# More first halves of the experts ahead of the gates, their results parked in DRAM: a two-layer PEER backbone on one core

## The chip, the cores and the metric

One core of one Trainium2 chip runs the whole program in one launch. The metric is the device time of one execution in microseconds, lower is better; the time of a kernel is the median of its runs.

## What is computed

The reference is a two-layer backbone over 256 latent tokens and 256 context tokens of width 1024. Each layer has an attention mixer and then a PEER channel mixer; the change touches the PEER part alone. For each token PEER picks 8 x 16 of 16384 experts, each an input vector `u` and an output vector `v`, and a gate for each pick:

```
def peer(h, w_q, sub_keys, u, v):
    q = (h @ w_q).reshape(T, 8, 2, 128)
    s = einsum('thpd,hpnd->thpn', q, sub_keys)
    sv, si = top_k(s, 16)
    cand = sv[:, :, 0, :, None] + sv[:, :, 1, None, :]
    fv, fi = top_k(cand.reshape(T, 8, 256), 16)
    idx = i1 * 128 + i2
    g = softmax(fv)
    act = gelu(einsum('td,ted->te', h, u[idx]))
    return einsum('te,ted->td', g * act, v[idx])
```

In layer 0 it runs over all 512 tokens, in layer 1 over the 256 latent ones.

## The kernel before

The kernel does not gather the picked experts (but for one block of tokens). It computes all 16384 experts for its tokens and multiplies by a dense matrix of gates that is zero where an expert was not picked. The experts are cut into 128 blocks of 128. For block i there are two halves:

- `first(i)` (line 755 on): load `u` (512 KB), split it into a high and a low bf16 half on ACT and DVE (`halves`, lines 101 and 102), 24 matmuls into a PSUM bank `tr` (`project`, line 282), and a Gelu on ACT (line 768) that writes `ga`, the activations of 128 experts for n tokens. In layer 0 n is 384, in layer 1 it is 256.
- `second(i)` (line 770 on): load `v` (512 KB), split it (lines 775 and 776, ring `vv` of four), for every eighth block load the gates `gq` from DRAM (line 779), multiply `ga` by the gates into `wf` (DVE, line 781), split that into `wh` (ACT) and `wl` (DVE), and 18 matmuls of 512 columns (12 in layer 1) into accumulators (line 791).

A first half needs only the normed tokens `h2`. A second half needs the gates, which `dense_gates` builds (lines 728 to 744): one-hot products on DVE (`oh`, `go`), small matmuls into banks `sc` and `pv`, copies into `stage` on ACT, and a 1 MB store `gd` per 16 tokens (24 stores in layer 0, 16 in layer 1). The first half does not wait for this, so some run while DVE builds gates: `PRE` (18 in layer 0, 32 in layer 1) have a buffer of their own for `ga`, `PARKED` (10 and 16) put it into `xT`, whose content lies in DRAM for that time. The others share a ring of four buffers `ga`.

The fourth block of 128 tokens in layer 0 goes another way: 128 indirect DMAs on POOL's queue (line 908) fetch 1 MB of expert rows each, and DVE multiplies and sums them (lines 914 and 920) beside layer 0's dense stage. So do the `wm` tiles of the modulation (line 160).

No order is written by hand. A scheduler takes the program, instruction by instruction, and fixes for each engine and each DMA queue one order, in which the chip then issues; a buffer of a ring is handed on when its last reader is done. All DMAs but the indirect ones are issued by SP, one queue, in order: a DMA that waits holds those behind it. "Gates" below is the stage in which gates are built, "dense" the one that follows, until the layer's last second half.

Of the kernel before, what the change touches and what calls it, by code (L numbers as in the profile page):

```python
# [9 lines left out]
F32 = mybir.dt.float32  # L10
# [8 lines left out]
P = 128  # L19
# [29 lines left out]
def program(ctx: ExitStack, tc: tile.TileContext, a, out):  # L49
    nc = tc.nc  # L50
    V, A, T, G = nc.vector, nc.scalar, nc.tensor, nc.gpsimd

    def pool(name, stack, bufs=1, side=None):
        return stack.enter_context(tc.tile_pool(name=name, bufs=bufs, side=side, reuse_waits="tile"))
# [5 lines left out]
    def bank(tag):  # L60
        return ps.tile([P, 512], F32, name=tag, tag=tag, bufs=2)
# [31 lines left out]
    def halves(t, shape, dt, keep=None):  # L93

        if dt == BF:
            hl = wk.tile([P, 2] + shape[1:], BF, name="half", tag="half", bufs=4) if keep is None else keep
            h, l = hl[:, 0], hl[:, 1]
        else:
            h = wk.tile(shape, dt, name="half", tag="half", bufs=4)
            l = wk.tile(shape, dt, name="half", tag="half", bufs=4)  # L100
        A.activation(h, t, AF.Copy)  # L101
        V.tensor_tensor(l, t, h, op=OP.subtract)  # L102
        return h, l
# [96 lines left out]
    def advance(steps, n):  # L200
        for _ in range(n):
            next(steps, None)
# [75 lines left out]
    def project(w, src, t0, n, p):  # L278

        for c in range(NC):  # L280
            for i, j in ((0, 0), (0, 1), (1, 0)):
                T.matmul(p[:, :n], w[i][:, c], src[j][:, c, t0:t0 + n], start=(c == 0 and i + j == 0), stop=(c == NC - 1 and i == 1))  # L282
# [465 lines left out]
    def dense(layer, n, h2, gd, dp, up, pre, extra, done):  # L748
        nt = n // P
        held = []  # L750
        acc = [[bank(("pv", "sc", "mm")[t]) for _ in range(2)] for t in range(nt)]
        gas, gqs = {}, {}
        flat = xT.rearrange("p c t -> p (c t)")

        def first(i):
            u = st.tile([P, NC, P], F32, name="u4", tag="u4", bufs=RING["u4"])
            nc.sync.dma_start(u, a[f"u{layer}"][i])
            w = halves(u, [P, NC, P], BF)
            p = bank("tr")
            project(w, h2, 0, n, p)  # L760
            if i < PRE[layer]:
                gas[i] = pre.tile([P, n], F32, name=f"ga{i}")
            elif i < PRE[layer] + PARKED[layer]:
                x = i - PRE[layer]
                gas[i] = flat[:, x * n:(x + 1) * n]
            else:
                gas[i] = up.tile([P, n], F32, name="ga", bufs=4)
            A.activation(gas[i], p[:, :n], AF.Gelu)  # L768

        def second(i):  # L770
            v = st.tile([P, D], F32, name="v4", tag="v4", bufs=RING["v4"])
            nc.sync.dma_start(v, a[f"v{layer}"][i * P:(i + 1) * P])
            vv = dp.tile([P, 2, D], BF, name="vv", bufs=HELD)
            vh, vl = vv[:, 0], vv[:, 1]
            A.activation(vh, v, AF.Copy)  # L775
            V.tensor_tensor(vl, v, vh, op=OP.subtract)  # L776
            if i % OCT == 0:
                gqs[0] = dp.tile([P, n // TB, OCT, TB], F32, name="gq", bufs=2)
                nc.sync.dma_start(gqs[0], gd[:, i // OCT].rearrange("p b (i t) -> p b i t", t=TB))
            wf = dp.tile([P, n], F32, name="wf", bufs=2)  # L780
            V.tensor_tensor(wf.rearrange("p (b t) -> p b t", t=TB), gas[i].rearrange("p (b t) -> p b t", t=TB), gqs[0][:, :, i % OCT], op=OP.mult)  # L781
            wh = dp.tile([P, n], BF, name="wh", bufs=max(HELD, 3))
            A.activation(wh, wf, AF.Copy)  # L783
            wl = dp.tile([P, n], BF, name="wl", bufs=HELD)
            V.tensor_tensor(wl, wf, wh, op=OP.subtract)  # L785

            def products(t):
                s = slice(t * P, (t + 1) * P)
                for w, v in ((wh, vh), (wh, vl), (wl, vh)):
                    for x in range(2):  # L790
                        T.matmul(acc[t][x], w[:, s], v[:, x * 512:(x + 1) * 512], start=(i == 0 and w is wh and v is vh),  # L791
                                 stop=(i == NK - 1 and w is wl))

            if i < NK - HELD:
                for t in range(nt):
                    products(t)
            else:
                held.append(products)

        for i in range(NK + AHEAD):  # L800
            if i < NK:
                first(i)
            if i >= AHEAD:
                second(i - AHEAD)
                extra(i - AHEAD)

        for t in reversed(range(nt)):
            for products in held:
                products(t)
            done(t, acc[t])  # L810
# [11 lines left out]
    PRE = (18, 32)  # L822
    PARKED = (TT * NC // (3 * P), TT * NC // SEQ)
    AHEAD = 2
    HELD = 4
    MODS = (8, 112)
    LAG = 4
    GATHERED = NK - 9
# [4 lines left out]
    with ExitStack() as layer0:  # L833
# [24 lines left out]
        up = pool("up0", r0, 2, side="right")  # L858
# [67 lines left out]
        def beside(i):  # L926
# [20 lines left out]
            if FRONT <= i < NK - 2:  # L947
                with tc.high_priority():
                    advance(early[0], 1)
            if i >= MODS[0]:  # L950
                advance(steps, 80 * (i + 1 - MODS[0]) // MODS[1] - 80 * (i - MODS[0]) // MODS[1])

# [30 lines left out]
        def front_(t, acc):  # L983
            with tc.high_priority():
                front(t, acc)
        dense(0, 3 * P, h2, gd, dp, up, pre, beside, front_)
        r0.close()
        hT, keys_values, attend = f1[1:]
# [9 lines left out]
    with ExitStack() as layer1:  # L998
        keep = pool("keep1", layer1)
        up = pool("up1", layer1, 2)  # L1000
# [65 lines left out]
        def finish(t, acc):  # L1066
# [15 lines left out]
            for g, y in enumerate(ys):  # L1082
                gs = slice(g * 512, (g + 1) * 512)
                V.scalar_tensor_tensor(y, y, r, fg[:, gs], op0=OP.mult, op1=OP.mult)
                nc.sync.dma_start(out[t * P:(t + 1) * P, gs], y)

        dense(1, SEQ, h2, gd, dp, up, pre, beside, finish)


# [86 lines left out]
```

## Time and profile before

| what | us |
|---|---|
| median of 3 runs | 2619.19 (2616.99 to 2622.06) |
| the profiled execution, its own time | 2624.13 |
| its span, first to last instruction | 2622.3 |
| PE busy | 2454.3 (94%) |
| DVE busy | 2142.3 (82%) |
| ACT busy | 1218.7 (46%) |
| gates of layer 0, about | 540 to 745 |
| dense of layer 0, about | 745 to 1560 |
| gates of layer 1, about | 1937 to 2061 |
| dense of layer 1, about | 2074 to 2611 |

Times along the program are microseconds from the span's start. A view by windows gives for each stretch the busy time of each engine (with the number of its instructions), the granted clock of TensorE as a share of 2.4 GHz, the busy share of the 16 DMA engines and the rate that they moved. A matmul's weights are loaded on PEld, beside PE.

### The profile page before, as it was taken

What the parts mean: (1) busy time and instruction counts of PE and PEld (TensorE: products, weight loads), DVE (VectorE), ACT (ScalarE), POOL (GpSimd) and SP (SyncE); (2) the same over time, 40 slices, a digit from 0 to 9 for tenths busy, and PEclk for the clock granted to TensorE, in tenths of its full rate; (3) what the DMA queues carried; (4) which work ended last, traced back from release to release, by engine and by line L of the source; (5) the groups of instructions that cost most, each with busy time, mean ns of one, the idle gap of its engine ahead of it and who ended that gap; (6) DMA issues with size and microseconds to landing.
All of it is one profiled execution on the core that took longest, in us unless ns stands there. A gap on an engine that the chain in (4) does not pass through costs nothing.

```text
span 2622.3 us, 41821 instructions
## 1 busy us (share of the span) xinstructions
PE 2454.3 (94%) x15600; PEld 1570.8 (60%) x15600; DVE 2142.3 (82%) x4820; ACT 1218.7 (46%) x2117; POOL 196.4 (7%) x132
## 2 busy tenths in 40 slices
PE   6989899999679999999999998798999699999998
PEld 2866479766534555555555555667888445666665
DVE  5975649999988999999988886977998787666665
ACT  3334535445433444444443334555565445555554
POOL 0000000000000212233222210000000000000000
PEclk8989899999679999999999999999999899999999
DMA  7631205556789999999999863701578977777762
GB/s 262 213 101 33 88 36 196 163 184 190 206 323 344 344 371 376 354 407 374 372 363 349 333 228 122 237 13 59 185 221 254 320 268 259 238 231 220 234 217 80
DMA packets 221000, 614.09 MB, mean 234 GB/s; under 512 B 16758, under 2 KB 104312, under 8 KB 199804
## 3 DMA queue, kind: packets, MB, share of 16 engines
q1 hardware_dynamic: 202364, 477.19, 53.5%
q0 software_dynamic: 18432, 134.23, 13.2%
q8 instruction: 122, 2.00, 0.3%
q14 instruction: 82, 0.67, 0.1%
HBM read 565.21 MB, written 46.15 MB: 233 GB/s over the span
## 4 chain that ended last, share of the span: by engine, by line
PE 71%; DVE 19%; DMA 5%; issue 2%; ACT 2%; SPq 0%; DVEq 0%; ACTq 0%
PE tr L282 23%; PE sc L791 12%; PE pv L791 12%; PE mm L282 8%; PE mm L791 6%; DVE half L102 4%; DVE go L733 3%; PE sc L385 2%; PE tr L292 2%; DVE oh L728 1%; PE pv L549 1%; PE mm L320 1%; PE sc L320 1%; PE sc L532 1%; DMA u<-in_u 1%
## 5 line engine op out<-in xcount | busy, mean ns | idle before, releaser
L282 PEld LDWEIGHTS <-half 128*128 128x128 bf16 x7488 | 723.9, 98 | 287.6 <-issue 10.8
L282 PE MATMUL tr<-h,half 128*128 128x384 bf16 (+1 forms) x6144 | 877.7, 300 | 4.6 <-ACT xT L768 2.0
L791 PEld LDWEIGHTS <-wh 128*128 128x128 bf16 x2560 | 251.5, 98 | 315.7 <-ACT wh L783 33.5
L102 DVE TENSOR_TENSOR half<-u,half 128x1024 bf16<-128x1024 f32 (+1 forms) x300 | 365.2, 1218 | 65.8 <-ACT half L101 64.9
L775 ACT ACTIVATE vv<-v 128x1024 bf16<-128x1024 f32 x256 | 269.3, 1055 | 277.5 <-issue 73.5
L776 DVE TENSOR_TENSOR vv<-v,vv 128x1024 bf16<-128x1024 f32 x256 | 312.3, 1221 | 102.7 <-ACT vv L775 101.7
L101 ACT ACTIVATE half<-u 128x1024 bf16<-128x1024 f32 (+1 forms) x300 | 315.2, 1051 | 105.1 <-DMA u<-in_u 43.9
L791 PE MATMUL pv<-vv,wh 128*128 128x512 bf16 x1024 | 269.7, 382 | 35.2 <-ACT wh L783 32.1
L908 POOL DMA_INDIRECT uv<-in_uv,idx x128 | 196.2, 1533 | 1347.4 <-DVE wf L781 753.1
L791 PE MATMUL sc<-vv,wh 128*128 128x512 bf16 x1024 | 269.5, 382 | 0.0
L768 ACT ACTIVATE ga<-tr 128x384 f32<-128x384 f32 (+1 forms) x230 | 100.5, 437 | 317.2 <-PE tr L282 315.2
L791 PEld LDWEIGHTS <-wl 128*128 128x128 bf16 x1280 | 125.5, 98 | 153.1 <-issue 2.1
L160 DVE CUSTOM_DVE_ANT_0 junk<-wm,silu_c 128x1024 bf16<-128x1024 f32 x160 | 194.8, 1218 | 1.8 <-DMA wm<-in_w_mod 1.0
L781 DVE TENSOR_TENSOR wf<-ga,gq 128x384 f32<-128x384 f32 (+1 forms) x230 | 111.8, 490 | 96.2 <-ACT ga L768 84.1
L783 ACT ACTIVATE wh<-wf 128x384 bf16<-128x384 f32 (+1 forms) x256 | 117.9, 463 | 131.2 <-DVE wf L781 62.6
L920 DVE SCALAR_TENSOR_TENSOR acc<-uv,wgt,acc 128x1024 f32<-128x1024 f32 x127 | 162.6, 1280 | 2.0
L914 DVE CUSTOM_DVE_ANT_0 uv<-uv,ht 128x1024 f32<-128x1024 f32 x128 | 155.6, 1217 | 0.3 <-DMA uv<-in_uv,idx 0.3
L791 PE MATMUL pv<-vv,wl 128*128 128x512 bf16 x512 | 153.2, 381 | 0.9 <-DVE wl L785 0.9
L791 PE MATMUL sc<-vv,wl 128*128 128x512 bf16 x512 | 152.9, 380 | 0.0
L282 PE MATMUL mm<-h,half 128*128 128x256 bf16 (+1 forms) x1248 | 137.4, 271 | 11.1 <-ACT h L274 3.5
L282 PE MATMUL mm<-hT,half 128*128 128x512 f32 (+1 forms) x672 | 140.1, 362 | 6.6 <-ACT hT L274 3.1
L791 PE MATMUL mm<-vv,wh 128*128 128x512 bf16 x512 | 134.4, 381 | 0.0
(275 smaller groups left out, 2758.6 us busy)
## 6 DMA issues: line engine op xcount, KB each, us to landing
u<-in_u SPq DMA_DIRECT2D x256, 512.0 KB
v<-in_v SPq DMA_DIRECT2D x256, 512.0 KB
wm<-in_w_mod SPq DMA_DIRECT2D x80, 512.0 KB
gd<-stage SPq DMA_DIRECT2D x40, 1024.0 KB
gq<-gd SPq DMA_DIRECT2D x16, 1536.0 KB
gq<-gd SPq DMA_DIRECT2D x16, 1024.0 KB
u<-in_w_pq SPq DMA_DIRECT2D x24, 512.0 KB
v<-in_w_pq SPq DMA_DIRECT2D x24, 512.0 KB
```

Of the source, the lines that this page charges most:

```text
L101: A.activation(h, t, AF.Copy)
L102: V.tensor_tensor(l, t, h, op=OP.subtract)
L160: mod_last[0] = order(V.tensor_tensor_reduce(junk, w, sc[:, s], 1.0, 0.0, OP.mult, OP.add, mods[layer][:, k, j, s:s + 1]))
L282: T.matmul(p[:, :n], w[i][:, c], src[j][:, c, t0:t0 + n], start=(c == 0 and i + j == 0), stop=(c == NC - 1 and i == 1))
L775: A.activation(vh, v, AF.Copy)
L776: V.tensor_tensor(vl, v, vh, op=OP.subtract)
L781: V.tensor_tensor(wf.rearrange("p (b t) -> p b t", t=TB), gas[i].rearrange("p (b t) -> p b t", t=TB), gqs[0][:, :, i % OCT], op=OP.mult)
L783: A.activation(wh, wf, AF.Copy)
L791: T.matmul(acc[t][x], w[:, s], v[:, x * 512:(x + 1) * 512], start=(i == 0 and w is wh and v is vh), stop=(i == NK - 1 and w is wl))
L908: dma = G.indirect_dma_start(out=uv[:], out_offset=None, in_=a["uv0"], in_offset=bass.IndirectOffsetOnAxis(ap=idx[:, k:k + 1], axis=0))
L914: keep_order(V.tensor_tensor_reduce(uv[:, :D], uv[:, :D], ht, 1.0, 0.0, OP.mult, OP.add, act3[:, k:k + 1]))
L920: V.scalar_tensor_tensor(acc3, uv[:, D:], wgt3[:, k:k + 1], acc3, op0=OP.mult, op1=OP.add)
```

## The change

After the `PRE` and `PARKED` blocks, the next 16 first halves of layer 0 and the next 8 of layer 1 no longer leave their result in the ring until their second half: it is stored to a DRAM tile `sent` right after the Gelu, and `second(i)` reads the result of block i + 1 back into a buffer of the same ring of four.

```
--- before.py
+++ after.py
@@ dense
         flat = xT.rearrange("p c t -> p (c t)")
+        sent = tc.dram_tile([P, SENT[layer], n], F32, name=f"sent{layer}")
 
         def first(i):
...
             else:
                 gas[i] = up.tile([P, n], F32, name="ga", bufs=4)
             A.activation(gas[i], p[:, :n], AF.Gelu)
+            x = i - PRE[layer] - PARKED[layer]
+            if 0 <= x < SENT[layer]:
+                nc.sync.dma_start(sent[:, x], gas.pop(i))
 
         def second(i):
+            x = i + 1 - PRE[layer] - PARKED[layer]
+            if 0 <= x < SENT[layer]:
+                gas[i + 1] = up.tile([P, n], F32, name="ga", bufs=4)
+                nc.sync.dma_start(gas[i + 1], sent[:, x])
             v = st.tile([P, D], F32, name="v4", tag="v4", bufs=RING["v4"])
...
     HELD = 4
+    SENT = (16, 8)
```

So blocks 28 to 43 of layer 0 (196,608 bytes each way) and 48 to 55 of layer 1 (131,072 bytes each way) take the new path: 24 stores and 24 read-backs on SP's queue. Lines from 754 on stand 1 to 9 further down in the changed kernel (768 becomes 769, 772 becomes 780).

What the scheduler made of it is seen at three places. The first is ACT in the gates of layer 0, where the last Gelus ahead of the dense stage stand (`stage` is a copy of gates, `half` the split of a `u`). Before, the fourth and last buffer of the ring is `ga_8638`, the result of block 31:

```order
L768 ACTIVATE ga_8638<-tr_8613 128x384
L101 ACTIVATE half_8893<-u4_8891 128x1024
L743 ACTIVATE stage_5730<-sc_5767 128x128x4
L743 ACTIVATE stage_5730<-pv_5777 128x128x4
L743 ACTIVATE stage_5806<-sc_5812 128x128x4
L743 ACTIVATE stage_5806<-pv_5822 128x128x4
L101 ACTIVATE half_8964<-u4_8962 128x1024
L101 ACTIVATE half_9039<-u4_9037 128x1024
L743 ACTIVATE stage_5806<-sc_5837 128x128x4
L743 ACTIVATE stage_5806<-pv_5847 128x128x4
```

With the change, the same place (`ga_8646` is block 31, `ga_8716` block 32):

```order
L769 ACTIVATE ga_8646<-tr_8621 128x384
L101 ACTIVATE half_8913<-u4_8911 128x1024
L743 ACTIVATE stage_5730<-sc_5767 128x128x4
L743 ACTIVATE stage_5730<-pv_5777 128x128x4
L743 ACTIVATE stage_5806<-sc_5812 128x128x4
L743 ACTIVATE stage_5806<-pv_5822 128x128x4
L769 ACTIVATE ga_8716<-tr_8691 128x384
L101 ACTIVATE half_8987<-u4_8985 128x1024
L101 ACTIVATE half_9065<-u4_9063 128x1024
L743 ACTIVATE stage_5806<-sc_5837 128x128x4
L743 ACTIVATE stage_5806<-pv_5847 128x128x4
```

One more Gelu stands there, and none follows until the dense stage. Counted over the whole of ACT's order, 33 Gelus now stand ahead of the last `stage` copy of layer 0 where 32 stood, and 53 where 52 stood in layer 1; one split of a `u` (lines 101 and 102) and one group of 24 matmuls per layer move with them.

The second place is SP's queue at the same time. With the change, from the second of these stores on (the numbers on `ga` tell buffers apart: 8500 is written by block 29, 8568 by 30, 8646 by 31, 8716 by 32; 8571, 8649 and 8719 are read back for blocks 29, 30 and 31, and block 28 was read back just before):

```order
L772 DMA sent0_6697<-ga_8500 128x384
L744 DMA gd0_4093<-stage_5660 2048x1x128
L758 DMA u4_8985<-in_u0 128x1024
L778 DMA ga_8571<-sent0_6697 128x384
L772 DMA sent0_6697<-ga_8568 128x384
L772 DMA sent0_6697<-ga_8646 128x384
L778 DMA ga_8649<-sent0_6697 128x384
L744 DMA gd0_4093<-stage_5730 2048x1x128
L758 DMA u4_9063<-in_u0 128x1024
L758 DMA u4_9137<-in_u0 128x1024
L772 DMA sent0_6697<-ga_8716 128x384
L778 DMA ga_8719<-sent0_6697 128x384
```

Five stores and four read-backs stand in the gates of layer 0 between the `gd` stores and `u` loads that stood there alone. The four read-backs (blocks 28 to 31) take all four buffers of the ring, long before their second halves come.

The third place is SP in the dense stage of layer 0, about where second halves 23 to 29 are worked off. Before (`v4_8500` is the `v` of block 27):

```order
L171 DMA wm_10458<-in_w_mod 128x1024
L772 DMA v4_8431<-in_v0 128x1024
L772 DMA v4_8500<-in_v0 128x1024
L772 DMA v4_8565<-in_v0 128x1024
L171 DMA wm_10606<-in_w_mod 128x1024
L171 DMA wm_10819<-in_w_mod 128x1024
L772 DMA v4_8640<-in_v0 128x1024
L772 DMA v4_8707<-in_v0 128x1024
```

With the change (`v4_8505` is the `v` of block 27, `ga_8791` the result of block 33, `ga_8794` block 32 read back):

```order
L772 DMA sent0_6697<-ga_8791 128x384
L780 DMA v4_8433<-in_v0 128x1024
L780 DMA v4_8505<-in_v0 128x1024
L171 DMA wm_10655<-in_w_mod 128x1024
L780 DMA v4_8573<-in_v0 128x1024
L778 DMA ga_8794<-sent0_6697 128x384
L171 DMA wm_10868<-in_w_mod 128x1024
L772 DMA sent0_6697<-ga_8869 128x384
L778 DMA ga_8872<-sent0_6697 128x384
L780 DMA v4_8651<-in_v0 128x1024
L780 DMA v4_8721<-in_v0 128x1024
L772 DMA sent0_6697<-ga_8941 128x384
```

The other 11 stores (blocks 33 to 43) and 12 read-backs (32 to 43) of layer 0 stand here, among the `v` loads; in layer 1 three stores and four read-backs stand in the dense stage.

## Rows read from the trace of the kernel before

**Rows 1.** The page's parts 1 and 2, whole span.

```profile
PE 2454.3 (94%) x15600; PEld 1570.8 (60%) x15600; DVE 2142.3 (82%) x4820; ACT 1218.7 (46%) x2117; POOL 196.4 (7%) x132
PE   6989899999679999999999998798999699999998
...
DVE  5975649999988999999988886977998787666665
...
PEclk8989899999679999999999999999999899999999
```

**Rows 2.** Windows by stage: busy us of each engine, clock, DMA share, GB/s.

```profile
core 0: us, PE busy (x) PEld busy (x) DVE busy (x) ACT busy (x) POOL busy (x), PEclk, DMA share, GB/s
...
650.00:745.00 95.00, 55.12 (x489) 43.76 (x487) 88.17 (x229) 39.00 (x65) 0.00 (x0) 0.66 0.73 216
...
850.00:1150.00 300.00, 300.00 (x1599) 156.28 (x1598) 299.60 (x456) 125.60 (x205) 79.35 (x48) 1.00 0.95 368
1150.00:1560.00 410.00, 410.00 (x2214) 216.44 (x2212) 366.41 (x521) 163.94 (x288) 108.62 (x73) 1.00 0.92 351
1990.00:2055.00 65.00, 58.41 (x603) 51.78 (x601) 57.87 (x93) 36.70 (x64) 0.00 (x0) 0.93 0.85 264
2055.00:2075.00 20.00, 3.45 (x35) 2.38 (x35) 7.22 (x13) 7.08 (x12) 0.00 (x0) 0.67 0.89 304
...
2300.00:2600.00 300.00, 299.64 (x2087) 204.65 (x2085) 180.83 (x232) 154.07 (x231) 0.00 (x0) 1.00 0.65 208
```

**Rows 3.** Waits of PE in the dense stage of layer 0, 750 to 1560.

```profile
PE pv L791 <- DVE vv L776: 1.7, 1, 1.7
PE pv L791 <- ACT vv L775: 1.2, 1, 1.2
```

**Rows 4.** Windows of 10 us, the same columns.

```profile
660.00:670.00 10.00, 5.41 (x67) 4.53 (x65) 10.00 (x20) 4.09 (x7) 0.00 (x0) 0.81 0.81 240
...
760.00:770.00 10.00, 10.00 (x48) 4.50 (x46) 9.87 (x16) 4.70 (x6) 0.00 (x0) 1.00 1.02 412
...
840.00:850.00 10.00, 8.26 (x41) 3.88 (x40) 10.00 (x16) 2.65 (x5) 2.68 (x2) 1.00 0.82 283
...
940.00:950.00 10.00, 10.00 (x58) 5.44 (x56) 10.00 (x20) 4.07 (x9) 1.40 (x1) 1.00 1.02 423
```

**Rows 5.** Waits in the gates of layer 0, 540 to 748 (total, times, longest).

```profile
PEld L741 <- DVE go L733: 30.5, 23, 9.3
...
PE pv L791 <- ACT wh L783: 14.7, 1, 14.7
...
ACT stage L743 <- DMA gd<-stage: 6.3, 3, 2.7
```

**Rows 6.** Costliest groups by form, whole span: the split of `u`.

```profile
L102 DVE TENSOR_TENSOR half<-u,half 128x1024 bf16<-128x1024 f32 x280 | 340.7, 1218 | 57.7 <-ACT half L101 56.7 <-issue 0.4
```

**Rows 7.** SP's issues at the end of layer 0's gates, in order of time.

```profile
728.21 4.54 SPq L744 DMA_DIRECT2D gd<-stage  x2
732.91 2.05 SPq L130 DMA_DIRECT2D silu_c<-silu  x1
738.11 0.81 SPq L779 DMA_DIRECT2D gq<-gd  x2
```

**Rows 8.** Waits around the end of layer 1's gates, 2000 to 2110.

```profile
PE pv L791 <- ACT wh L783: 16.0, 1, 16.0
...
DVE wf L781 <- DMA gq<-gd: 8.1, 1, 8.1
...
ACT stage L743 <- DMA gd<-stage: 6.0, 2, 4.0
```

**Rows 9.** Waits in the dense stage of layer 0, 870 to 1010.

```profile
ACT vv L775 <- DMA v<-in_v: 9.4, 7, 4.0
ACT vv L775 <- PE mm L791: 8.4, 7, 2.1
DVE uv L914 <- DMA uv<-in_uv,idx: 0.3, 1, 0.3
```

## The prediction

> **What bounds the kernel now.** I read the page's busy rows and slices first, then windows by stage, then who waits in each. PE is busy 94% of the span at a granted clock near full, and its slices of 65.6 us dip, beside the start and layer 1's attention (slices 25 to 28), in slices 11 and 12, the end of layer 0's gates, and in slice 32, the end of layer 1's [rows 1]. So the question is one of stages. In the dense stage of layer 0 PE is busy without a gap from 850 on, at 2.4 GHz (clock 1.00) [rows 2], and between 750 and 1560 it waits 2.9 us in all [rows 3]. That stage is bound by PE. DVE is as full there until 1150 (299.6 of 300 us), and the DMA engines are close behind with a share of 0.95 [rows 2]: three resources stand side by side, PE ahead by a little. In the gates of layer 0 it is the other way round. DVE is busy 10.00 of 10 us [rows 4], PE stands and waits for DVE's `go` (30.5 us in all) [rows 5], and from 650 to 745 PE is busy 55.12 of 95 us at a mean clock of 0.66 [rows 2]. That is the room the change aims at: a first half moved there should cost PE nothing and relieve the dense stage.
>
> **What a first half is worth.** From 1150 to 1560 PE issued 2214 matmuls, 185 ns each [rows 2]; a block has 24 + 18 = 42 of them, so 7.78 us. Second halves alone run at 48 matmuls in 10 us, 208 ns each [rows 4], so 18 take 3.75 us. The first half is the rest, 4.0 us. In layer 1 the rate is 300 / 2087 = 144 ns [rows 2], a block of 24 + 12 is 5.17 us, and both halves stream the same number of columns (24 x 256 and 12 x 512), so a first half is 2.6 us. What it costs where it goes is the split of `u` on DVE, 1.22 us [rows 6], because DVE sets the pace of the gates. The split and the Gelu on ACT lie beside that: ACT is busy 39 of 95 us [rows 2].
>
> **How many move.** The orders of the two kernels answer this, and not with 16 and 8. One Gelu more stands ahead of the last gates in each layer, 33 for 32 and 53 for 52. The reason is the ring. The read-back of block i + 1 has nothing to wait for but its store and a free buffer, so the scheduler issues the read-backs of blocks 28 to 31 inside the gates; they fill all four buffers of `ga` and keep them until second halves 28 to 31 have read them. Block 33 then has no buffer before second half 28, deep in the dense stage. The detour through DRAM gives back four of the buffers it was to save; what is gained is the one result (block 32, and 52 in layer 1) that lies in DRAM alone.
>
> **The sum.** Layer 0's dense stage loses one first half: -4.0 us. Its gates gain one split on DVE: +1.2. Layer 1's dense stage: -2.6. Its gates: +1.2, since DVE is nearly full there too (57.87 of 65 us) [rows 2].
>
> The 24 stores and 24 read-backs cost DMA time, and SP's order. In the gates of layer 0 five stores and four read-backs are 9 x 0.197 = 1.77 MB in a stretch whose DMA share is 0.73 [rows 2]: hidden in the free quarter. A read-back there holds SP until its store has landed, and a `gd` store behind it is late, which holds ACT's next `stage` copy (it waits for that 6.3 us already [rows 5]). The trace has no store of this size. The nearest is the last `gd` store, 1 MB, issued by about 732.2, after which SP could issue the `gq` load at 738.1 [rows 7], so at most 5.9 us for one. A store of gates goes out every 205 / 24 = 8.5 us, which covers such a wait. I take 0, with 5.9 as the upper end.
>
> At the end of layer 1's gates the cover is thinner. PE waits 16.0 us there for the first second half, DVE 8.1 us for `gq`, ACT 6.0 us for `gd` stores [rows 8]: the last stores end the stage. Nine transfers of 0.131 MB and one `u` of 0.52 MB come on top, 1.70 MB; the DMA engines moved 304 GB/s at a share of 0.89 there [rows 2], 342 when full, so between 0 and 5.0 us. Of these only the `u` load stands among the last three `gd` stores; I take its 1.5 us.
>
> In the dense stage of layer 0 eleven stores and twelve read-backs are 4.52 MB, and they come while second halves 28 to 45 run, some 17 blocks of 7.78 us, 132 us. At the best rate, 423 GB/s at a share of 1.02 [rows 4], they take 10.7 us of all DMA engines. The free share is 5% [rows 2], 6.6 us. So between 0 and 10.7 us. I take 0: from 870 to 1010 ACT waited 8.4 us, seven times, for PE to free a buffer of `vv` [rows 9], so `v` was up to four blocks ahead of PE, and a load that lands some us later is not yet felt. The Trainium skill (DMA: Bandwidth & Descriptors, Specifications) puts the limit from HBM at about 358 GB/s for a core. This trace disagrees: 368 GB/s over 300 us. By that figure the stage would be DMA-bound already and the whole 4.52 MB would be added, an estimated 12.6 us, against the 0 that I take.
>
> SP's order adds waits as well. The store of block 33 stands ahead of the `v` loads of blocks 26, 27 and 28, and waits for a Gelu that waits for a buffer. But that buffer is freed by `wf` of block 28, and DVE's split of `v` 23, for which the load of `v` 26 waits anyway, stands right behind it on DVE. Some tenths of a microsecond, inside the same lead of `vv`: 0. In layer 1's dense stage PE is busy 299.64 of 300 us with DVE at 180.83 and DMA at 0.65 [rows 2], so seven small transfers are hidden; the cover is DVE's free 40%.
>
> Together: -4.0 + 1.2 - 2.6 + 1.2 + 1.5 = -2.7 us. The profiled execution took 2624.13 us by its own time (span 2622.3) and would take 2621.4; it lies 4.9 above the median of the runs, 2619.19, which becomes **2616.5 us**. That is 0.1%, and about 0.2% (5.2 us) is what a measurement of this kernel can tell from no change. I forecast no change.
>
> **Rivals.** *The DMA engines fill up* (slower). The 4.52 MB find no room, `v` and gathered rows land late, and DVE, which now waits 0.3 us for a gather in 140 us [rows 9], waits for them; with DVE full there is nothing to catch up with before 1150. For it: ACT already waits 9.4 us for `v` in that stretch [rows 9]. Against it: the lead of `vv`, and windows that reach 1.02. It decides once the lead is used up. This is also what a limit of 358 GB/s would do (the Trainium skill, DMA: Bandwidth & Descriptors, Specifications), and the 368 GB/s measured speak against it. Price from the rows: the whole 10.7, so 2616.5 + 10.7 = 2627.2 us. Chance 0.22, and 0.02 more for the held SP queue in the gates on top of it (5.9 us).
>
> *PE's holes close too* (faster). Before block 34 PE has few first halves to put between seconds; from 840 to 850 it issued 41 matmuls for 48 [rows 4], and that is where its 2.9 us of waiting lie [rows 3]. In the new order one more first half is in hand there. If those waits go and the end of layer 1's gates does not suffer, 2616.5 - 2.9 - 1.5 = 2612.1 us. Against it: DVE is full right there, and a wait for it returns elsewhere. Chance 0.22.
>
> *The change does what its words say*: all 16 and 8 run ahead, 16 x (4.0 - 1.2) + 8 x (2.6 - 1.2) = 56 us, so 2563 us. PE's idle 40 us in 650 to 745 [rows 2] would allow most of it, but the order is fixed before the chip sees it: 0.02.
>
> **How the numbers follow.** No change, around 2616.5: 0.52. Faster 0.22 + 0.02 = 0.24, slower 0.22 + 0.02 = 0.24. The likeliest case alone spans 2612 to 2623 (its unknown terms: 1.5 less to 5.9 more, and the scatter of runs). The range reaches down past the closed holes and up past the full DMA engines with the held queue, 2627.2 + 5.9: 2607 to 2633.
>
> **What would show it.** Right: 33 and 53 Gelus ahead of the last `stage` copies; the first second half of layer 0 about 1 us later; PE still without waits in the dense stage, and that stage about 4 us shorter; the DMA share from 870 to 1010 near 1.00 without consequences. Wrong: waits of PE for `wh`, `vv` or `wl` between 860 and 1010, DVE idle behind a gather or `v`, SP waiting for a store while `v` loads stand behind it, or a gates stage longer by more than 2 us.

## The result, and the profile after

The changed kernel took 2637.2 us (median of 5 runs, 2632.32 to 2639.94) against 2622.06 us for the kernel before in the same session (5 runs, 2616.99 to 2625.52): a ratio of 1.0062, 95% interval [1.0051, 1.0073]. It is 0.6% slower, 15 us, where no change was forecast at 2616.5 us and the range ended at 2633. The profiled execution took 2635.86 us by its own time (span 2634.1), 11.8 us of span more than the one of before. The profile of before is of a run 2.1 us above its median and that of after of one 1.3 us below; hence 11.8 where the medians differ by 15.

Where those 11.8 us lie is read from two kinds of instruction in the timeline: the copies into `stage` (first one of each layer) and the matmuls of the second halves (first and last start of each layer). Layer 0's last second half starts at 1617.9 us before, so "dense 0" reaches past the 1560 at which the windows of [rows 2] end.

| stretch, us | before | after | difference | forecast |
|---|---|---|---|---|
| start to the first `stage` copy of layer 0 | 543.7 | 541.2 | -2.5 | 0 |
| gates 0: to the first second half | 202.5 | 203.7 | +1.2 | +1.2 |
| dense 0: to the last second half | 871.7 | 881.4 | **+9.7** | **-4.0** |
| attention of layer 1 | 321.2 | 320.1 | -1.1 | 0 |
| gates 1 | 134.9 | 140.3 | **+5.4** | **+2.7** |
| dense 1 | 537.1 | 536.2 | -0.9 | -2.6 |

The loss has two places, the dense stage of layer 0 and the gates of layer 1. The first stretch lies ahead of all that the change touches.

The page's parts 1 and 2 after, to be laid beside [rows 1]:

```profile
PE 2450.2 (93%) x15600; PEld 1568.5 (60%) x15600; DVE 2144.8 (81%) x4820; ACT 1216.9 (46%) x2117; POOL 198.5 (8%) x132
...
PE   5999899999679989999999998899999699999998
...
PEclk8989899999689999999999999999999799999999
```

PE is busy as long as before, but for 4 us. What is new is a slice of 8 at 14 (counted from 0: 922 to 988 us), in a stage where [rows 1] has a 9. The windows by stage after (the two of layer 1's gates begin 7 us later, and the second of them is 6 us longer), beside [rows 2]:

```profile
650.00:745.00 95.00, 53.78 (x495) 41.92 (x493) 88.12 (x229) 39.04 (x67) 0.00 (x0) 0.68 0.76 232
850.00:1150.00 300.00, 288.45 (x1510) 148.16 (x1509) 295.61 (x449) 118.71 (x199) 83.89 (x48) 0.99 0.95 375
1150.00:1560.00 410.00, 410.00 (x2216) 216.54 (x2214) 361.71 (x509) 162.54 (x284) 105.37 (x73) 1.00 0.92 350
1997.00:2062.00 65.00, 57.32 (x592) 51.09 (x590) 54.73 (x88) 35.32 (x61) 0.00 (x0) 0.95 0.82 256
2062.00:2088.00 26.00, 7.75 (x79) 6.14 (x77) 12.19 (x19) 9.61 (x17) 0.00 (x0) 0.59 0.97 324
2300.00:2600.00 300.00, 299.64 (x2080) 204.09 (x2079) 183.88 (x233) 155.45 (x233) 0.00 (x0) 1.00 0.68 216
```

From 850 to 1150 PE was busy all 300 us before and is busy 288.45 us now, with 1510 matmuls for 1599. The DMA share is the same 0.95. The waits of PE in the dense stage of layer 0 (750 to 1560), 2.9 us in [rows 3]:

```profile
PE pv L799 <- ACT wh L791: 11.6, 4, 4.9
PE pv L799 <- ACT vv L783: 1.2, 1, 1.2
PE tr L282 <- ACT ga L769: 0.3, 1, 0.3
```

So PE waits four times for `wh`, the high half of the gated result, which ACT makes from DVE's `wf`. The 10-us windows show where, and what DVE did meanwhile (compare 940:950 in [rows 4]):

```profile
930.00:940.00 10.00, 9.50 (x54) 5.09 (x52) 10.00 (x15) 1.69 (x4) 2.23 (x2) 1.00 1.02 424
940.00:950.00 10.00, 6.30 (x25) 2.85 (x26) 10.00 (x17) 3.90 (x7) 2.03 (x2) 0.83 1.02 417
...
980.00:990.00 10.00, 5.61 (x21) 2.42 (x22) 9.84 (x18) 3.77 (x9) 0.00 (x0) 0.83 0.91 369
```

In the windows in which PE stands, DVE is busy 10.00 and 9.84 of 10 us. It hardly waits; it is doing something else first. DVE's timeline between two `wf` (start, duration, instruction) says what:

```profile
925.08 0.55 DVE L789 TENSOR_TENSOR wf<-ga,gq 128x384 f32<-128x384 f32 x1
...
928.04 1.21 DVE L102 TENSOR_TENSOR half<-u,half 128x1024 bf16<-128x1024 f32 x1
...
930.87 1.27 DVE L929 SCALAR_TENSOR_TENSOR acc<-uv,wgt,acc 128x1024 f32<-128x1024 f32 x1
932.07 1.21 DVE L923 CUSTOM_DVE_ANT_0 uv<-uv,ht 128x1024 f32<-128x1024 f32 x1
...
934.43 1.21 DVE L102 TENSOR_TENSOR half<-u,half 128x1024 bf16<-128x1024 f32 x1
...
939.06 1.21 DVE L102 TENSOR_TENSOR half<-u,half 128x1024 bf16<-128x1024 f32 x1
940.20 1.21 DVE L160 CUSTOM_DVE_ANT_0 junk<-wm,silu_c 128x1024 bf16<-128x1024 f32 x1
...
942.54 0.54 DVE L789 TENSOR_TENSOR wf<-ga,gq 128x384 f32<-128x384 f32 x1
```

For 17.5 us, more than two blocks of 7.78 us, no `wf` comes, but three splits of `u` for first halves, and gathers (`uv`, `acc`), `wm` tiles (`junk`) and splits of `v`. Counted from 745 to 945, the groups by form of the kernel before (first) and of the changed one:

```profile
L781 DVE TENSOR_TENSOR wf<-ga,gq 128x384 f32<-128x384 f32 x32 | 17.4, 550 | 3.5 <-DMA gq<-gd 3.5
L781 DVE TENSOR_TENSOR wf<-xT,gq 128x384 f32<-128x384 f32 x10 | 5.5, 555 | 0.2
```

```profile
L789 DVE TENSOR_TENSOR wf<-ga,gq 128x384 f32<-128x384 f32 x28 | 15.2, 549 | 0.0
L789 DVE TENSOR_TENSOR wf<-xT,gq 128x384 f32<-128x384 f32 x10 | 5.5, 553 | 0.1
```

In that window 42 blocks were gated before and 38 after, at the same 0.55 us each; two more of the changed kernel's lie ahead of 745, so by 945 it is 42 against 40. The distance still grows: `wf` of block 43 starts at 956.6 us before and at 983.2 after. These instructions did not become slower; their order is another one. Summing DVE's instructions in their order, from the stage's first `wf` on, each at the mean of its row (1.22 us for a split, a `uv` and a `junk`, 1.27 for an `acc`, 0.55 for `wf` and `wl`), 232 us of work stand ahead of `wf` of block 43 before, and 260 us after. (Their own times in the two traces add up to 226 and 253 us: the same difference, but for 1 us.) PE's work ahead of that block's products (4.0 and 3.75 us a half) is 209 and 217 us. DVE is asked for 28 us more, PE for 8. In the traces the additional instructions are five splits of `u`, two of `v`, six `junk`, three `uv` and five `acc`. They came with first halves that run further ahead: at that place the splits of `u` are ten blocks ahead of `wf`, where they were four ahead.

In layer 1's gates the wait at the end did not grow: beside [rows 8],

```profile
PE pv L799 <- ACT wh L791: 15.4, 1, 15.4
...
DVE wf L789 <- DMA gq<-gd: 8.3, 1, 8.3
...
ACT stage L743 <- DMA gd<-stage: 5.6, 3, 2.9
```

From the last `stage` copy to the first second half it is 14.3 us for 14.1. The 5.4 us lie ahead of that copy, where SP and ACT wait (the waits of SP from 1960 to 2080 and of ACT from 1980 to 2076):

```profile
SPq L778 <- DMA sent<-ga: 6.4, 3, 3.6
...
ACT half L101 <- DMA u<-in_u: 22.7, 10, 7.2
```

Line 778 is the read-back: SP stands three times until the store has landed, with `u` loads behind it. ACT's wait for `u` in these 96 us was about half as long before:

```profile
ACT half L101 <- DMA u<-in_u: 12.1, 6, 5.0
```

### The profile page after: what moved, and what is told of

Its sections match the earlier page's. It is cut to its first block, busy times and chain, and to the rows that moved or that the text cites. A ratio compares the mean times of both kernels' runs of the same rounds, so it can differ in the third digit from the quotient of the medians.

```text
span 2634.1 us, 41906 instructions
## 1 busy us (share of the span) xinstructions
PE 2450.2 (93%) x15600; PEld 1568.5 (60%) x15600; DVE 2144.8 (81%) x4820; ACT 1216.9 (46%) x2117; POOL 198.5 (8%) x132
## 4 chain that ended last, share of the span: by engine, by line
PE 50%; DVE 12%; DMA 6%; issue 3%; ACT 2%; SPq 0%; DVEq 0%; ACTq 0%
PE tr L282 20%; PE sc L799 10%; PE pv L799 9%; PE mm L799 5%; DMA v<-in_v 4%; DVE half L102 2%; PE mm L282 2%; DVE go L733 1%; PE pv L549 1%; DVE junk L160 1%; DVE vv L784 1%; PE sc L532 1%; DMA u<-in_u 1%; DMA gd<-stage 1%; DVE oh L728 1%
## 5 line engine op out<-in xcount | busy, mean ns | idle before, releaser
L282 PE MATMUL mm<-h,half 128*128 128x256 bf16 (+1 forms) x1248 | 137.5, 271 | 11.6 <-DVE half L102 4.0
```

## The experiments

Theory O: in layer 0 it is the order on DVE, which has other work ahead of `wf`. Rival B: it is the 4.5 MB more through full DMA engines. For layer 1: SP's queue, against the extra split and bytes. All runs, by the same milestones; the kernel before had medians of 2620.3 to 2621.1 us beside them. A median is of all runs of a kernel, the stages are of its one profiled execution. Layer 0 repeats well: gates and dense stage together are 1074.0 to 1074.2 us in the three kernels whose layer 0 is that of before, and 1085.1 in both that have the changed one. The dense stage of layer 1, where nothing was changed in it, was 537.1 and 536.1.

| run | median | ratio, 95% interval | gates 0 | dense 0 | attention | gates 1 | dense 1 |
|---|---|---|---|---|---|---|---|
| sent_layer0_only | 2633.91 | 1.0050 [1.0037, 1.0064] | 203.8 | 881.2 | 321.4 | 134.8 | 536.1 |
| sent_layer1_only | 2624.64 | 1.0016 [1.0007, 1.0025] | 202.5 | 871.7 | 320.6 | 141.2 | 534.5 |
| same_hoist_few_bytes | 2623.11 | 1.0008 [0.9999, 1.0017] | 203.1 | 866.1 | 324.9 | 142.6 | 537.5 |
| same_bytes_no_hoist | 2641.91 | 1.0076 [1.0063, 1.0090] | 208.7 | 875.5 | 327.6 | 140.9 | 535.7 |
| ring_of_five | 2619.14 | 0.9992 [0.9983, 1.0001] | 202.9 | 865.9 | 325.0 | 137.8 | 535.4 |
| order_repaired | 2634.46 | 1.0048 [1.0035, 1.0061] | 196.4 | 879.3 | 329.6 | 140.7 | 538.8 |
| layer1_other_queues | 2619.72 | 0.9998 [0.9989, 1.0007] | 202.0 | 871.9 | 321.3 | 136.6 | 534.2 |
| read_backs_own_ring | 2606.70 | 0.9949 [0.9936, 0.9963] | 223.7 | 843.6 | 324.5 | 143.6 | 518.5 |
| few_bytes_changed_order | 2638.86 | 1.0066 [1.0052, 1.0080] | 203.1 | 882.4 | 321.9 | 142.8 | 538.3 |
| all_bytes_other_order | 2636.27 | 1.0062 [1.0048, 1.0076] | 203.1 | 872.4 | 326.2 | 140.8 | 536.4 |
| ring5_and_layer1_own_ring | 2611.61 | 0.9961 [0.9948, 0.9975] | 202.7 | 866.0 | 325.1 | 140.2 | 521.2 |
| own_ring_other_queues | 2605.98 | 0.9940 [0.9926, 0.9953] | 210.1 | 852.4 | 328.5 | 142.5 | 524.0 |
| other_order_other_queues | 2629.35 | 1.0033 [1.0021, 1.0044] | 202.8 | 872.3 | 330.0 | 137.9 | 532.5 |
| changed_other_queues | 2634.70 | 1.0056 [1.0043, 1.0069] | 202.8 | 882.8 | 323.2 | 136.4 | 535.8 |

**The two layers apart.**

```
-    SENT = (16, 8)
+    SENT = (16, 0)        # sent_layer0_only
+    SENT = (0, 8)         # sent_layer1_only
```

> SENT = (16, 0): the change in layer 0 alone. In the changed kernel's profile layer 0 gave +1.1 us in the gates and +8.7 in the dense stage, layer 1 +5.5 and -1.0. If the layers do not act on each other, this kernel is about 10 us slower than the kernel before, its dense stage of layer 0 near 880 us with PE waits of some 12 us, its gates of layer 1 back at about 135 us. If the loss were a general slowing (DRAM traffic, drift of a run), layer 1 would stay long too.

> SENT = (0, 8): the change in layer 1 alone. By the changed kernel's profile +5.5 us in the gates of layer 1 and -1.0 in the dense stage after them: about 4.5 us slower than before, and a dense stage of layer 0 as before, near 871 us with PE waits of about 3 us.

Near enough to what was expected: 12.8 us (about 10 expected) and 3.5 us slower by their medians, together 16.3, about the changed kernel's loss (15 us), and each in the stages named. The layers can be studied one by one. In layer 1 alone the dense stage gains 2.6 us, as forecast.

**The bytes alone, and the first halves alone.** First the same stores and read-backs with 16 of 384 columns (of 256 in layer 1):

```
+        sent = tc.dram_tile([P, SENT[layer], TB], F32, name=f"sent{layer}")
+                nc.sync.dma_start(sent[:, x], gas.pop(i)[:, :TB])
+                nc.sync.dma_start(gas[i + 1][:, :TB], sent[:, x])
```

> The same stores and read-backs, but of 16 columns each (8 KB for 197 KB); the second halves of the blocks concerned multiply those 16 columns, repeated, so their results are not the reference's. The splits of u still run 6 to 8 blocks ahead of wf on DVE between blocks 36 and 51 (4 before, up to 10 in the changed kernel). Theory 'order' (DVE is full there, and what runs ahead puts wf, then wh, then PE back): PE still waits 5 to 12 us for wh between 900 and 1000, dense stage of layer 0 876 to 880 us. Rival 'bytes' (4.5 MB more through full DMA engines): the waits go back to about 3 us and the stage is at or under 871 us. In the gates of layer 1, bytes: +5.5 falls to about +2.6; SP order: +5.5 stays.

Layer 0 (gates and dense stage) takes 1069.2 us instead of 1085.1, and PE's waits for `wh` are gone from 750 to 1560:

```profile
PE pv L800 <- ACT vv L783: 1.2, 1, 1.2
PE tr L282 <- ACT ga L769: 0.3, 1, 0.3
```

That is what rival B expected. But the run does not separate them as I had thought: with smaller transfers the scheduler also makes another order, in which 248 us of DVE work stand ahead of `wf` of block 43 and not 260. In layer 1's gates the loss is still there, 7.7 us (142.6 for 134.9), and SP's wait for the small stores is the same 6.4 us: there it is not the bytes. The other way round, the kernel before with the traffic added:

```
+            if 0 <= x < SENT[layer]:
+                nc.sync.dma_start(sent[:, x], gas[i])
...
+                nc.sync.dma_start(up.tile([P, n], F32, name="gb", bufs=1), sent[:, x])
```

> The kernel before, with every store of the change and a read-back into a scratch buffer that nobody reads: the same 4.7 MB in layer 0 and 2.1 MB in layer 1, but the order of the halves as before (the split of u 4 blocks ahead of wf from block 35 to 50). Theory 'order': dense stage of layer 0 near 871 us, PE waits about 3 us, total within 3 us of before. Rival 'bytes': dense stage 878 to 882 us, PE or DVE waits of 7 to 11 us more between 870 and 1010. In the gates of layer 1 the transfers alone: 0 to +5.5 us.

Neither expectation met it. The dense stage is 3.8 us longer, between the two theories, and 6.2 us are lost where neither looked, in the gates of layer 0. From 620 to 745 SP stood 16.3 us in four read-backs, twice the 8.3 in two of the changed kernel:

```profile
SPq L777 <- DMA sent<-ga: 16.3, 4, 5.3
```

The gates of layer 1 are 6.0 us longer without any first half more, and the attention before them 6.4; the total is 20.8 us longer than before. So the stores and read-backs have a price of their own when nothing runs ahead. That the 6.2 us are these waits was not shown by a run. The read-backs share one scratch buffer here, so they can also wait for each other.

**The extra first half without DRAM.**

```
-                gas[i] = up.tile([P, n], F32, name="ga", bufs=4)
+                gas[i] = up.tile([P, n], F32, name="ga", bufs=5)
```

> The kernel before with five buffers of ga instead of four and nothing sent to DRAM: the same one first half more ahead of the gates in each layer (33 and 53 Gelus). My forecast's terms without the DRAM traffic: -4.0 and -2.6 in the dense stages, +1.2 and +1.2 in the gates, so -4.2 us, about 0.2%. By the runs so far the dense stage of layer 0 should come out near 866 us, as with few bytes; the gates of layer 1 near 136 us, not 141, if it is the stores and read-backs in SP's queue that lengthen them, and near 141 us if it is the extra first half itself.

Layer 0's dense stage is 865.9 us, the expected 866 and 5.8 less than before: the 4.0 us of one first half, 1.4 us of PE's waits that closed (2.9 to 1.5), and 0.4 that I cannot place. The gates of layer 1 take 137.8, between the two expectations. The total is 2 us better, within what can be told from no change, since the attention of layer 1 gave 4 us back.

**Order against bytes, all four cases.** A first try moved the gathers and `wm` tiles later in the program and held the splits of `u` behind an earlier `wf`:

```
+            with tc.issue_after(wfs[i - 5].ins) if layer == 0 and 33 <= i < 80 else nullcontext():
+                w = halves(u, [P, NC, P], BF)
+        def lagged(i):
+            return i - min(max(i - 33, 0), 5, max((80 - i) // 4, 0))
```

> The changed kernel with all its DRAM traffic, but on DVE the split of u of blocks 33 to 79 is queued behind wf of five blocks earlier, and the gathers and wm tiles of these blocks come up to five blocks later in the program. By the order of DVE, the work ahead of wf of block 43 is 249 us (before 232, changed 260, few bytes 248) and PE's work ahead of that block's products 221 us (209, 217, 217). Theory 'order on DVE': PE's waits for wh in the dense stage of layer 0 fall from 11.6 to under 3 us and the stage from 881 to 867 to 872 us, though all bytes still move. Rival 'bytes': still 10 us of waits or more and 878 us or more.

The waits for `wh` fell from 11.6 to 3.3 us, near the "under 3" of theory O. The stage did not come out as expected, 879.3, because work left the gates as well (196.4 us): 33 splits of `u` stand ahead of the first second half there and 39 in the changed kernel, and six splits of 1.22 us are the 7.3 us that the gates are shorter. The sum of the two stages is 1075.7, 9.4 less than in the changed kernel. Since this kernel differs in more than one thing, two others followed that force DVE's instructions from `wf` 33 to `wf` 52 into a given order:

```
+        traced = {i.name: i for i in nc.cur_bb.bb.instructions}
+        chain_ = [traced[f"I-{k}"] for k in DVE_ORDER]
+        for one, two in zip(chain_, chain_[1:]):
+            tc.add_manual_dep(two, one.name, ...)
```

> The kernel with 16 columns stored and read back (second halves of those blocks multiply them repeated), with DVE's instructions from wf of block 33 to wf of block 52 forced into the order that they have in the changed kernel; PE's order follows it from block 41 on. The work ahead of wf of block 43 is 260 us on DVE, 217 on PE, as in the changed kernel; few bytes alone had 248 and 217. Theory 'order': PE waits 10 to 12 us for wh near 940 to 990, gates and dense stage of layer 0 together 1079 to 1083 us (few bytes 1069, changed kernel 1085). Rival 'bytes': as few bytes, 1069 to 1071 us and waits of 1.5 us.

> The changed kernel with all its bytes, with DVE's instructions from wf of block 33 to wf of block 52 forced into the order of the kernel with few bytes (248 us of DVE work ahead of wf of block 43 instead of 260). Theory 'order': gates and dense stage of layer 0 together 1070 to 1074 us instead of 1085, PE waits for wh under 4 us. Rival 'bytes': 1082 to 1085 us and the waits stay above 8 us, now behind DVE's waits for v, uv or ga.

Gates and dense stage of layer 0 together, in us:

| | order with few bytes (248 us ahead) | order of the change (260 us ahead) |
|---|---|---|
| 16 columns moved | 1069.2 | 1085.5 |
| all bytes moved | 1075.5 | 1085.1 |

Few bytes in the changed order lose 16.3 us, as much as lies between few bytes and the changed kernel (15.9), and its waits are back:

```profile
PE pv L800 <- ACT wh L792: 11.8, 2, 6.9
PE pv L800 <- ACT vv L783: 1.2, 1, 1.2
```

That shows theory O: with hardly any bytes, DVE's order alone makes the loss. (DVE's order is what is forced; PE, ACT and SP then come out in other orders too.) With all bytes the better order is 6.3 us longer than with few, the worse one is not: there DVE is late anyway. These 6.3 us I put down to the bytes and what waits for them. They are not that alone for certain, since the order of the first halves is not the same in the two kernels: ahead of `wh` of block 40, 42 Gelus stand in ACT's order with few bytes and 44 with all. So the second expectation was met in size (9.6 us less) but 1.5 us above its range, and PE's waits for `wh` were 6.0 us and not under 4:

```profile
PE pv L799 <- ACT wh L791: 6.0, 3, 2.3
```

Of the 6.3 us one wait of DVE shows 3.4, in the waits of `all_bytes_other_order` from 750 to 1560; in the changed kernel it is 0.3:

```profile
DVE wf L789 <- DMA ga<-sent: 3.4, 1, 3.4
```

Its total did not fall with it, 2636.27 us for 2637.2. In the profiled executions the attention of layer 1 took 326.2 us for 320.1, so 6.1 of the 9.6 us were given back there. In the total the order is seen with few bytes (2638.86 against 2623.11) and, by 5 us, in the pair with other queues below (2634.70 against 2629.35). The profiled execution with all bytes and the better order is 3.4 us under its median, that with few bytes 4.2 above; where a kernel's executions differ, one profile does not show.

**SP's queue.** The same DMAs, other queues:

```
-                nc.sync.dma_start(sent[:, x], gas.pop(i))
+                nc.scalar.dma_start(sent[:, x], gas.pop(i))
-                nc.sync.dma_start(gas[i + 1], sent[:, x])
+                G.dma_start(gas[i + 1], sent[:, x])
```

> SENT = (0, 8) as before, but the stores are issued by ACT and the read-backs by POOL; the order on SP is otherwise the same. If the +6 us in the gates of layer 1 come from SP, which stands 6.4 us behind read-backs that wait for their store, while u loads queue behind it: 135 to 137 us instead of 141, total about 4 us under the run with SENT = (0, 8). If they come from the extra split on DVE and the extra bytes: still 140 to 141 us.

> All bytes and the DVE order of the kernel with few bytes, as in all_bytes_other_order, but stores issued by ACT and read-backs by POOL. If the 6 us that are left in layer 0 are SP's queue: gates and dense stage of layer 0 together 1069 to 1072 us. If they are the bytes: 1074 to 1077 us. POOL also issues the gathers; if a read-back there holds gathers back, more than 1077. Layer 1's gates 136 to 138 us instead of 141.

> The changed kernel as it is, DVE's order in layer 0 unchanged (260 us of work ahead of wf of block 43), but stores issued by ACT and read-backs by POOL in both layers. Theory 'order on DVE' for layer 0 and 'SP's queue' for layer 1: layer 0 stays at 1080 to 1085 us with PE waits of 10 to 13, the gates of layer 1 fall from 140.3 to 136 to 138 us, the total by about 4. Rival, 'SP's queue' in layer 0 too: 1074 us or less there.

In layer 1 the gates fall from 141.2 to 136.6 us (from 140.3 to 136.4 in the changed kernel). DVE's order in that stage is the same to the instruction, and so are ACT's and SP's but for the moved DMAs. The read-backs wait as before, and longer, but on a queue with only read-backs behind them:

```profile
POOL ga L778 <- DMA sent<-ga: 15.8, 3, 9.9
```

That shows it for layer 1: stores and read-backs that waited held SP, and SP held the `u` loads. The two moved together, so how the 4.6 us divide between them is not shown. The Trainium skill (Trainium Kernel Development and Optimization, Key Constraints) says that DMAs issued from SP, ACT and POOL share the same 16 engines and that issuing from several only saves the sequencer's issue time. The gates of layer 1 disagree: 4.6 us came from waits that no longer had loads behind them. In layer 0 the queue has no part. The better order with all bytes stays at 1075.1 us (1075.5 on SP), so its 6 us are not SP's queue. The changed order stays at 1085.6; the scheduler's order on DVE is not quite the same there, but its work ahead of `wf` of block 43 is (253.0 us in the trace for 253.2).

**Versions that beat both.** Read-backs with buffers of their own, so that they no longer take those of the first halves:

```
-                gas[i + 1] = up.tile([P, n], F32, name="ga", bufs=4)
+                gas[i + 1] = up.tile([P, n], F32, name="gb", bufs=2)
...
-                gas[i] = up.tile([P, n], F32, name="ga", bufs=4)
+                gas[i] = up.tile([P, n], F32, name="ga", bufs=3)
```

> The read-backs get a ring of their own (two buffers gb, and three ga), so that they no longer take the buffers of the first halves: 47 and 57 Gelus stand ahead of the gates' end (33 and 53 with the change). Rival 'as its words say': 14 first halves more at 4.0 - 1.2 us and 4 at 2.6 - 1.2, 45 us less, about 2590 us. Against it: DVE is full from 540 to 1150 us, so what PE no longer does before 1150 only lets it wait for DVE; then the stage is DVE's and the total lies between 2610 and 2640 us.

Now the change nearly does what its words say, 47 and 57 Gelus ahead (48 and 60 would be all). The kernel is 30 us faster than the changed one, where the rival had 45, and 14 us faster than before. The gates of layer 0 grow by 21.2 us, a bit more than 15 splits of 1.22; the dense stage loses 28.1 of 60. The windows say where the rest went:

```profile
850.00:950.00 100.00, 81.47 (x352) 35.42 (x358) 99.12 (x162) 31.26 (x53) 23.21 (x15) 0.97 0.94 363
950.00:1050.00 100.00, 95.21 (x493) 48.92 (x500) 100.00 (x156) 39.19 (x68) 28.33 (x16) 0.99 0.96 372
```

DVE is full, PE waits for it: the stage is DVE's there, as the "against it" had it. Layer 1, where DVE has room, gave 18.6 us of its dense stage for 8.7 in the gates: 59 Gelus stand ahead of its first second half, seven more than before, and seven first halves of 2.6 us are 18.2. Two more candidates joined the parts (a ring of five in layer 0 without DRAM, `SENT = (0, 8)`; and `SENT = (8, 8)` in both layers with other queues):

> A candidate: layer 0 as with the ring of five and no DRAM traffic; layer 1 with three buffers ga and a ring of two for the read-backs, stores issued by ACT, read-backs by POOL; 33 and 57 Gelus ahead. From the ring of five's 2619.1 us: the dense stage of layer 1 518.5 instead of 535.4 us as with the read-backs' own ring, its gates 139 instead of 137.8: about 2603 us.

> A candidate: both layers with three buffers ga, two for the read-backs, eight results each sent to DRAM, stores issued by ACT, read-backs by POOL; 39 and 57 Gelus ahead. Layer 1 as in the other candidate. In layer 0 six halves more in the gates at 1.2 us each on DVE, and 6 x 4.0 us less PE work in a dense stage in which DVE is full up to 1150 us: between as much as the ring of five (2603 us in all) and 17 us better (2587). If the read-backs in POOL's queue hold the gathers back, over 2606.7, the run with read-backs of their own on SP.

Both are faster than before and slower than expected: 2611.61 and 2605.98. The second is no better than `read_backs_own_ring` by more than can be told. Its layer 0 is 4.8 us shorter (1062.5 for 1067.3), and its attention of layer 1 4 us longer.

## Why the prediction was wrong

- **One first half more ahead in each layer**: right (33 and 53 Gelus), and so were its prices. Gates 0 +1.2 was forecast and measured. -4.0 in dense 0 shows where nothing else happens: -5.8 with the ring of five, of which 1.4 are the waits of rival "PE's holes close too". -2.6 in dense 1 is -2.6 and -2.9 in the two runs of layer 1 alone (-0.9 in the changed kernel; an unchanged layer 1 alone gave 1.0 of difference).
- **The step that failed** is the sum for layer 0's dense stage. It priced the bytes, SP's order and the loads of `v`, and covered all three with the lead of the ring `vv`. The order of DVE has no term in it. I had counted where Gelus stand ahead of the gates' end, found that block 33 gets a buffer only "deep in the dense stage", and stopped there. But from that point on a result that is stored frees its buffer as soon as it is stored, so first halves run up to ten blocks ahead of their second halves between blocks 36 and 47, and with them gathers and `wm` tiles. That this stage's DVE is full until 1150 stood in the prediction; that it therefore matters what stands first on it did not. The cover that I named holds `v`; it was `wf` that came late. Price: 16.3 us with few bytes, 9.6 with all. Of the signs that the prediction gave for being wrong, two came: waits of PE for `wh` between 860 and 1010, and a gates stage longer by more than 2 us.
- **4.52 MB at 0** (bounds 0 to 10.7): with the better order 6.3 us, inside the bounds (PE's order may have a part in it), and hidden in the changed kernel behind the late DVE. **SP's order in dense 0**: 0, right.
- **End of layer 1's gates, +1.5**: wrong in place and size. Its end grew by 0.2 us. The waits of stores and read-backs on SP, for which I had taken 0 in layer 0 because the stores of gates cover them, cost 3.9 to 4.6 us in layer 1, where the cover was not looked at. Without them the gates are 1.5 to 1.7 us longer than before; with the extra first half alone (the ring of five) 2.9, for which the prediction had 1.2.
- **Rival "the DMA engines fill up"** came nearest in time (2627.2) with a mechanism that the four cases do not bear out: with few bytes the loss is the same, and with the better order all bytes are 6.3 us longer, not 10.7. **"The change does what its words say"** did not happen here; where 15 and 7 first halves ran ahead it gave 14 us, and my price for that many is 15 x 2.8 + 7 x 1.4 = 52. In layer 0 7 us of 42 are left, because DVE, which is full there, sets the pace; in layer 1 it is the 10 us of the price, and 3 went in the attention of layer 1.

What stays open: why the scheduler put `wf` of these blocks behind so much other work was not tried. That it depends on the size of the transfers is seen in the orders (260 us with all bytes, 248 with few).

## What to carry to other kernels

Giving a buffer back early also lets work run ahead elsewhere: read the order on the fullest engine through the whole stage, and sum what stands ahead of the instruction that the critical engine waits for, not only at the place that the change is meant for. A read-back that can be issued early will be: give it buffers and a queue of its own, or it takes those that it was to free and holds the loads behind it. When two causes are tied by a scheduler (here bytes and order), force the order of one kernel upon the other and run all four cases.

## What the runs showed of the hardware

After the waits of 4.2 and 4.9 us, PE came back at half its clock. PE's timeline (the last column is the wait):

```profile
943.70 1.89 PE L799 MATMUL pv<-vv,wh 128*128 128x512 bf16 x4 [4.20 <-ACT wh L791]
945.38 1.90 PE L799 MATMUL sc<-vv,wh 128*128 128x512 bf16 x4
...
952.52 1.03 PE L799 MATMUL pv<-vv,wh 128*128 128x512 bf16 x4
953.39 1.03 PE L799 MATMUL sc<-vv,wh 128*128 128x512 bf16 x4
...
962.74 1.04 PE L799 MATMUL pv<-vv,wh 128*128 128x512 bf16 x4 [1.61 <-ACT wh L791]
```

Four matmuls of 512 columns take 1.68 us from start to start after the long wait and 0.87 a little later, 420 and 217 ns each: the levels of 1.2 and 2.4 GHz. After the wait of 1.61 us nothing was lost. The clock of 0.83 in the windows 940:950 and 980:990 above is this; the twelve products after each of the two long waits took 4.3 us instead of 2.6. So 11.6 us of waits cost 11.6 + 2 x 1.7 = 15.0 us, close to the 15.3 us between the dense stages of the changed kernel and of the one with few bytes.

The DMA engines of this one core moved 424 GB/s in a window of 10 us (930:940) at a share of 1.02. The Trainium skill (Perfetto Trace Analysis, Roofline) puts the ceiling of a single active core at its 16 DMA engines, about 435 GB/s. The trace agrees: it stays below that.

The attention stage of layer 1, which no edit touches, took 320 to 323 us in seven of the kernels and 324 to 330 in the other nine. The first 40 us of it before and with the ring of five:

```profile
1617.90:1657.90 40.00, 28.41 (x181) 25.50 (x180) 32.40 (x89) 22.43 (x45) 0.00 (x0) 0.87 0.47 151
```

```profile
1608.00:1648.00 40.00, 27.39 (x154) 25.17 (x153) 28.53 (x84) 20.12 (x41) 0.00 (x0) 0.79 0.45 147
```

Its instructions come in another order there, and the granted clock is 0.79 for 0.87. In six of the seven kernels DVE's and ACT's orders in this stage are those of the kernel before, to the instruction; in the other nine DVE's is another. So a change of order in one stage reaches into the next through the scheduler, and several gains of 4 to 10 us were given back in part in this way. Which instructions in that order cost the time was not tried; the clock alone does not tell, since it starts at 0.79 in two of the seven as well.
